# Opening a hand-synchronised section from ScalarE instead of SyncE in a batched matrix product

## The chip, the cores and the metric

The kernel runs on one NeuronCore of a Trainium2 chip. The metric is device time in microseconds (us) of one execution; for a series of runs the median is given. A profile of a single execution goes with it: its span runs from the first to the last instruction on the core.

## What is computed

Sixteen independent products of 512 x 512 matrices in float32, the first factor given transposed:

```
"a": np.random.randn(batch, k, m).astype(np.float32),     # batch = 16, k = m = n = 512
"b": np.random.randn(batch, k, n).astype(np.float32),
...
return np.matmul(a.transpose(0, 2, 1), b).astype(np.float32)
```

33.55 MB are read from HBM and 16.78 MB written.

## The kernel before

The batch is worked off in 8 pairs of 2 matrices. One pair of `a` (2 MB) or of `b` (2 MB) is one SBUF tile `x`; four such tiles (`NX = 4`) take turns. VectorE casts them to bfloat16 (`abf`, `bbf`, in two halves each), TensorE multiplies into four PSUM tiles (`ps`[...]), ScalarE copies PSUM to seven output tiles `o`, and these are stored to HBM. The first pair is treated specially: its first matrix alone is loaded in pieces of 256 KB and 768 KB per operand (lines 74 and 75), then the second in pieces of 1 MB (line 77), so that the first product can begin early. Its multiplications are those of line 135, all later ones those of line 155.

Nothing is left to the scheduler. All work of the five engines stands in one section, opened on line 72 by `tc.tile_critical`, in which every wait is written by hand on semaphores of the kernel's own (`s_x`, `s_cast`, `s_mm`, `s_ev`, `s_out` and so on). Within the section every engine runs its own list in order:

- SyncE issues all loads (lines 74 to 86) and the outputs of the first seven pairs (line 91), all on one DMA queue. The first eight loads wait for nothing; the later ones wait until VectorE is through with the tile (`s_in`). The outputs wait for the next to last load (`s_h`, line 88) and for ScalarE's `s_out` (line 90), so that stores come after the loads.
- VectorE: casts, lines 93 to 123.
- TensorE: two counted loops, lines 127 to 165.
- ScalarE: copies out of PSUM (lines 174 and 180) and a tiny write that raises `s_out` (line 185). The load of its function table, put in by the compiler, carries line 174 and is the first thing it does in the section.

The section itself has an opening and a closing. At the opening, one engine, the section's `sync_engine`, executes a NOP (line 72) that raises a semaphore, and every engine has a branch that waits for that semaphore before it enters. At the closing, the same engine raises another semaphore, each of the engines SyncE, ScalarE, VectorE and TensorE drains and reports, and the `sync_engine` collects the reports with semaphore waits and a last NOP, whose semaphore releases what comes after the section. No `sync_engine` is named on line 72, and the engine is SyncE then. Ahead of the opening lies a start barrier of all engines (line 207 in the profile); what follows the sections has line 218 (the end of the program's context).

After the section, a second one (line 188) with GpSimd as `sync_engine` waits for the outputs of the earlier pairs, and SyncE issues the output of the last pair (line 192). `tc.no_sync_barrier()` only keeps the order of the code; it makes no engine wait.

## Times and profile before

| quantity | before |
|---|---|
| median of 10 runs | 123.63 us (123.22 to 124.17) |
| the profiled execution | 123.62 us |
| its span | 121.9 us |
| mean granted TensorE clock | 0.854 |
| TensorE matmul busy | 62.2 us (51%) |
| VectorE busy | 38.0 us (31%) |
| ScalarE busy | 32.1 us (26%) |
| DMA, share of 16 engines | 97.6% |
| HBM traffic over the span | 413 GB/s |

How to read what is shown of the profile. Engines are PE (TensorE matmul), PEld (its weight load), DVE (VectorE), ACT (ScalarE), POOL (GpSimd), SP (SyncE); a "q" behind the name means the sequencer of that engine, which handles waits, branches, NOPs and the issue of DMAs, and isn't counted as busy. "L72" is line 72 of the kernel. The slices divide the span into 40 equal parts and give tenths of busy time. The chain that ended last goes back from the last instruction, each time to what released it. The timeline gives start and duration in us, and in brackets the idle time before and what ended it. In the views by stretches, the columns are named where they are shown.

### The profile page before, as it was taken

How to read it: one execution, taken by the hardware profiler on the slowest of the kernel's cores; microseconds unless marked ns; L12 is line 12 of the kernel's file. 1: busy time of each engine (PE TensorE's matmuls, PEld its weight loads, DVE VectorE, ACT ScalarE, POOL GpSimd, SP SyncE). 2: the span in 40 equal slices, each digit the busy share in tenths (PEclk: the TensorE clock that was granted, in tenths of full speed). 3: DMA queues.
4: the chain of work that ended last, by engine and by line, in shares of the span. 5: the costliest groups of instructions: out<-in, count | busy, mean ns of one | idle time of the engine just before them, and what ended most of it. 6: DMA issues, size and time to landing. Idle time of an engine off the chain costs nothing.

```text
span 121.9 us, 1209 instructions
## 1 busy us (share of the span) xinstructions
PE 62.2 (51%) x480; PEld 35.7 (29%) x480; DVE 38.0 (31%) x48; ACT 32.1 (26%) x41; POOL 0.2 (0%) x4
## 2 busy tenths in 40 slices
PE   0006928739969649979919928989900000000000
PEld 0002303326546334636606606646500000000000
DVE  0042070294494092474355437492000000000000
ACT  4000330510560830191570390191560000000000
POOL 0000000000000000000000000000000000000000
PEclk9999995999999995999999999999997555555555
DMA  3999999999999999999999999999999999999993
GB/s 95 365 425 428 468 430 430 430 430 430 430 430 430 430 430 430 430 430 436 430 430 430 436 430 401 422 430 428 428 428 430 430 428 428 428 428 430 430 428 161
DMA packets 5200, 50.33 MB, mean 413 GB/s; under 512 B 464, under 2 KB 464, under 8 KB 976
## 3 DMA queue, kind: packets, MB, share of 16 engines
q1 hardware_dynamic: 5200, 50.33, 97.6%
HBM read 33.55 MB, written 16.78 MB: 413 GB/s over the span
## 4 chain that ended last, share of the span: by engine, by line
DMA 51%; DVE 5%; PE 5%; ACT 3%; issue 2%; ACTq 0%; DVEq 0%
DMA x<-in_b_dram 36%; DMA x<-in_a_dram 9%; DMA out_dram<-o 6%; PE ps L135 5%; ACT o L180 3%; DVE bbf L117 2%; DVE abf L117 2%; DVE abf L98 1%; DVE done L123 0%; ACTq L72 0%; DVE bbf L98 0%; DVEq L116 0%
## 5 line engine op out<-in xcount | busy, mean ns | idle before, releaser
L155 PE MATMUL ps<-bbf,abf 64*128 64x512 bf16 x448 | 51.5, 386 | 12.9 <-PEq L150 12.9
L155 PEld LDWEIGHTS ps<-bbf,abf 64*128 64x128 bf16 x448 | 31.6, 112 | 32.8 <-issue 18.1
L180 ACT COPY o<-ps 128x1024 f32<-128x1024 f32 x28 | 26.3, 1027 | 38.9 <-PE ps L155 34.9
L117 DVE CAST abf<-x 128x2048 bf16<-128x2048 f32 x14 | 17.1, 1223 | 17.3 <-PE ps L155 11.9
L117 DVE CAST bbf<-x 128x2048 bf16<-128x2048 f32 x14 | 17.1, 1223 | 14.1 <-DMA x<-in_b_dram 14.1
L135 PE MATMUL ps<-bbf,abf 128*128 128x512 bf16 x32 | 10.7, 510 | 13.0 <-PEq L133 13.0
L135 PEld LDWEIGHTS ps<-bbf,abf 128*128 128x128 bf16 x32 | 4.1, 132 | 19.1 <-issue 18.0
L174 ACT COPY o<-ps 128x1024 f32<-128x1024 f32 x4 | 4.1, 1013 | 18.5 <-PE ps L135 18.5
L98 DVE CAST abf<-x 128x2048 bf16<-128x2048 f32 x2 | 2.5, 1226 | 12.0 <-PE ps L135 6.1
L98 DVE CAST bbf<-x 128x2048 bf16<-128x2048 f32 x2 | 2.4, 1224 | 1.6 <-DMA x<-in_b_dram 1.6
L185 ACT ACTIVATE done<-done 1x1 uint32<-1x1 uint32 x8 | 1.6, 197 | 0.0
L174 ACT ACT_TABLE_LOAD x1 | 1.3, 1283 | 0.9 <-SPq L72 0.9
L123 DVE MEMSET done<- 1x1 f32 x14 | 0.8, 59 | 0.0
L102 DVE MEMSET done<- 1x1 f32 x2 | 0.1, 59 | 0.0
L207 POOL MEMSET const-bfloat16-1.0<- 128x1 bf16 x1 | 0.1, 102 | 0.0
L207 POOL MEMSET const-uint8-127<- 128x1 uint8 x1 | 0.1, 102 | 0.0
L207 POOL MEMSET const-float32-1.0<- 128x1 f32 x1 | 0.1, 99 | 0.0
L207 POOL MEMSET const-float32-0.0<- 128x1 f32 x1 | 0.1, 98 | 0.2 <-issue 0.2
## 6 DMA issues: line engine op xcount, KB each, us to landing
out_dram<-o SPq DMA_DIRECT2D x8, 2048.0 KB, 21.8
x<-in_a_dram SPq DMA_DIRECT2D x7, 2048.0 KB, 12.1
x<-in_b_dram SPq DMA_DIRECT2D x6, 2048.0 KB, 15.9
x<-in_b_dram SPq DMA_DIRECT2D x3, 1024.0 KB, 13.5
x<-in_a_dram SPq DMA_DIRECT2D x1, 1024.0 KB, 8.4
x<-in_a_dram SPq DMA_DIRECT2D x1, 768.0 KB, 4.4
x<-in_b_dram SPq DMA_DIRECT2D x1, 768.0 KB, 6.4
x<-in_a_dram SPq DMA_DIRECT2D x1, 256.0 KB, 2.6
```

What stands on the lines that cost most here:

```text
L98: nc.vector.tensor_copy(out=bf_ts[0][:], in_=x_ts[j][:, u * RV:(u + 1) * RV, :]).then_inc(s_cast, 1)
L102: nc.vector.memset(dve_done[:, j:j + 1], 0.0).then_inc(s_in, 1)
L117: nc.vector.tensor_copy(out=(bbf_ts if n % 2 else abf_ts)[v][:], in_=x_ts[n % NX][:, v * RV:(v + 1) * RV, :],).then_inc(s_cast, 1)
L123: nc.vector.memset(dve_done[:, n:n + 1], 0.0).then_inc(s_in, 1)
L135: mm = nc.tensor.matmul(ps_ts[0][h][:, t % 2, :], a_m[:, r, t], bbf_ts[0][:, r, :], start=(r == 0), stop=(r == RV - 1),)
L155: mm = nc.tensor.matmul(ps_ts[g][h][:, t % 2, :], a_m[:, t], bbf_ts[v][rows, r, :], start=(v == 0 and r == 0), stop=(v == V - 1 and r == R ...
L174: nc.scalar.copy(out=o_ts[0][:, g, 2 * h:2 * h + 2, :], in_=ps_ts[0][h][:]).then_inc(s_ev[h], 1)
L180: ev = nc.scalar.copy(out=o_ts[i % NO][:, g, 2 * h:2 * h + 2, :], in_=ps_ts[g][h][:])
L185: nc.scalar.memzero(act_done[:, i:i + 1]).then_inc(s_out, 1)
L207: nc = _bacc.Bacc("TRN2", target_bir_lowering=False, num_devices=1)
```

## The change

One argument is added: the section's `sync_engine` is ScalarE (`EngineType.Activation`).

```diff
-    with tc.tile_critical(no_gpsimd_drain=True):
+    with tc.tile_critical(sync_engine=mybir.EngineType.Activation, no_gpsimd_drain=True):
         for j in range(2):
             nc.sync.dma_start(x_ts[j][:, 0:1, :], top_v[j]).then_inc(s_f[j], 16)
             nc.sync.dma_start(x_ts[j][:, 1:RV, :], low_v[j]).then_inc(s_f[j], 16)
```

## Prediction

> **What bounds the kernel now.** I read the granted clock and span first (one core, 121.9 us, clock 0.854), then the page's slices, then the chain that ended last, then the timeline of both ends of the span, and last the records of single instructions in the trace.

> The slices say that the DMA engines are the bound from about 2 us to 120 us.

> ```profile
> span 121.9 us, 1209 instructions
> ...
> PE 62.2 (51%) x480; PEld 35.7 (29%) x480; DVE 38.0 (31%) x48; ACT 32.1 (26%) x41; POOL 0.2 (0%) x4
> ...
> DMA  3999999999999999999999999999999999999993
> GB/s 95 365 425 428 468 430 430 430 430 430 430 430 430 430 430 430 430 430 436 430 430 430 436 430 401 422 430 428 428 428 430 430 428 428 428 428 430 430 428 161
> ...
> q1 hardware_dynamic: 5200, 50.33, 97.6%
> ```

> No compute engine is busy for more than half of the span, while the one DMA queue fills 97.6% of 16 engines. 50.33 MB at the steady 430 GB/s are 117.0 us of the 121.9. So the length is 117 us of transfer, plus what comes before the first packet, plus a slow ramp, plus the tail. Whatever moves the first packet moves everything behind it; whatever moves work that sits behind a full queue moves nothing.

> The first microseconds, from the timeline:

> ```profile
> 0.90 1.28 ACT L174 ACT_TABLE_LOAD   x1 [0.90 <-SPq L72]
> 0.94 0.39 SPq L74 DMA_DIRECT2D x<-in_a_dram  x1
> 1.39 0.42 SPq L75 DMA_DIRECT2D x<-in_a_dram  x1
> 1.86 0.42 SPq L74 DMA_DIRECT2D x<-in_b_dram  x1
> ```

> SyncE issues its first transfer at 0.94 us, and ScalarE was held until 0.90 by SyncE's line 72, the opening of the hand-made section. The two ends of the DMA stream, in stretches (columns: busy time of PE, PEld, DVE, ACT, POOL, then granted clock, DMA share, GB/s):

> ```profile
> 0.90:2.40 1.50, 0.00 (x0) 0.00 (x0) 0.00 (x0) 1.28 (x1) 0.00 (x0) 1.00 0.08 29
> 2.40:3.00 0.60, 0.00 (x0) 0.00 (x0) 0.00 (x0) 0.00 (x0) 0.00 (x0) 1.00 1.51 393
> 3.00:4.00 1.00, 0.00 (x0) 0.00 (x0) 0.00 (x0) 0.00 (x0) 0.00 (x0) 1.00 0.80 328
> 4.00:5.00 1.00, 0.00 (x0) 0.00 (x0) 0.00 (x0) 0.00 (x0) 0.00 (x0) 1.00 0.98 399
> 5.00:6.00 1.00, 0.00 (x0) 0.00 (x0) 0.14 (x1) 0.00 (x0) 0.00 (x0) 1.00 1.09 367
> 6.00:7.00 1.00, 0.00 (x0) 0.00 (x0) 1.00 (x1) 0.00 (x0) 0.00 (x0) 1.00 0.96 387
> 7.00:8.00 1.00, 0.00 (x0) 0.00 (x0) 0.08 (x1) 0.00 (x0) 0.00 (x0) 1.00 1.01 424
> ```

> Hardly a byte moves before about 2.2 us (first packet in the trace: 2.19), 1.25 us after the first issue. From there to 8 us the engines are never idle but below 430: 0.6 x 393 + 328 + 399 + 367 + 387 + 424 = 2,141 KB in 5.6 us, against 2,408 KB at 430, so 0.62 us is lost in the ramp.

> The close of the section, from the timeline of the end:

> ```profile
> 86.65 3.76 ACT o L180 x4
> 90.41 0.06 ACTq L72
> ...
> 90.60 3.64 SPq L192 DMA_DIRECT2D out_dram<-o  x1
> ```

> (the first two lines are the last of the chain). The last output is issued at 90.60 and lands, by the trace, 30.3 us later, at 120.93.

> [...]

> **The change part by part.** The records of the opening, in us from the span's start (not a view of the page, so given as I read them from the trace):

> ```
> 0.650 SP  semaphore wait (start barrier)    0.654 ACT the same
> 0.715 SP  NOP L72, 13 ns, raises the section's semaphore
> 0.751 ACT branch, waits for that semaphore
> 0.772 DVE branch, same    0.785 SP branch, same    0.812 PE branch, same
> 0.897 ACT table load      0.941 SP first DMA issue
> ```

> *Opening.* The change takes the NOP from SyncE and gives one to ScalarE; SyncE's branch then waits for ScalarE's semaphore. By SyncE's own spacing the NOP would fall on ScalarE 65 ns after its barrier wait: 0.654 + 0.065 = 0.719. SyncE's branch then comes when it hears of it. Three readings: as ScalarE heard SyncE (36 ns): 0.755; as GpSimd heard SyncE's NOP at the close (90.529 to 90.568, 39 ns): 0.758; as PE did (97 ns): 0.816. Against 0.785 that is -0.030, -0.027 or +0.031 us. SyncE can't come before 0.715, the place of its NOP, so the gain is at most 0.07 and, with the wait, 0.03. I take -0.03 us, because SyncE, like ScalarE and GpSimd, has short records (17 ns for a semaphore wait, PE 51). Bounds: -0.07 and +0.03. From branch to first issue (0.156 us) and from issue to issue (0.45 to 0.50 us) nothing changes, so all eight DMAs that follow (lines 74 to 83) move by the same amount, as does the first packet. This lies wholly on the path.

> *ScalarE's own part.* Its table load moves from 0.897 to about 0.95, by the extra NOP; it ends near 2.2, and the first copy (line 174) starts at 13.87, after 11.69 us of waiting for PE. Nothing, hidden by that wait; without the cover it would cost 0.05.

> *VectorE and PE.* Same instructions, released 4 ns later at 0.719. VectorE first works at 5.86, when data land; PE after that. Nothing.

> *Closing.* The gather of all engines moves too: ScalarE raises the closing semaphore, drains (1.089 us, started 89.415), then makes two semaphore waits and a NOP which now stand behind its own drain, where SyncE made its two waits beside it (89.587 and 89.646, NOP at 90.529). Two waits at some 0.06 us each and a hop to SyncE with its branch (0.04 to 0.15) put the issue of line 192 at about 90.8 to 90.9 in place of 90.60. Queued behind it on SyncE is only the final wait; GpSimd's line 188 also starts later by it, and then waits until 116.1 anyway. Its cover: six output transfers of 2 MB were still landing when line 192 was issued (outputs at about 91.5, 96.4, 101.3, 106.2, 111.1, 116.0), so 25 us of transfer stand ahead of it. Nothing, as long as the delay is below some 20 us; without cover it would cost 0.2 to 0.3.

> *Tail.* After the last landing (120.93) SyncE's last waits and the end barrier take 0.94 us, with the same kinds of waits; zero, bounds -0.07 and +0.07 (one wait more or less at the end).

> *Sum.* -0.03 us, with bounds -0.14 and +0.10. The profiled execution took 123.62 us, 121.87 of it span and 1.75 around it, which the change doesn't touch: 123.62 - 0.03 = 123.59. That execution is the median of the runs shown (123.63) to 0.01, so the forecast is 123.59. Differences under 0.2% (0.25 us) are about what a measurement of this kernel can tell from no change; the runs shown spread over 0.95 us, and a median of ten such can be off by 0.1 to 0.2.

> **The rivals.**
> *No effect:* SyncE hears of ScalarE as late as of itself, or as PE does: 123.62 to 123.65. For it: SyncE's branch came only 70 ns after its own NOP, and a hop has a price. Against: two hops of 36 and 39 ns.
> *The ramp falls out better:* another first moment gives another interleaving of the small first transfers (2 and 6 KB rows), and half of the 0.62 us is regained: 123.59 - 0.31 = 123.28. For it: the ramp is uneven (328, 399, 367 GB/s). Against: the order and spacing of the issues stay, and 30 ns is little beside 450.
> *Slower, ScalarE opens late:* ScalarE's lateness was covered by 11.69 us before; now each of its delays ahead of the NOP goes straight to the first DMA. It costs a measurable 0.25 us from the point where its NOP starts later than 0.719 + 0.03 + 0.25 = 1.00 us; if the table load (1.283 us) ran ahead of the NOP, SyncE's branch would come at 0.719 + 1.283 + 0.036 = 2.04, 1.25 later: 124.87. Against: in the changed program's order the NOP stands ahead of the table load, and ScalarE passed the start barrier 4 ns after SyncE. For: one execution is shown, and whether ScalarE is always so prompt isn't.

> **How the numbers follow.** Forecast 0.66, no effect 0.12, ramp better 0.14, ScalarE late 0.08. The forecast and "no effect" (0.78) are within 0.2%, but a draw of medians may carry about 0.06 of it past the bound downwards and 0.07 upwards. So faster 0.14 + 0.06 = 0.20; same 0.65; slower 0.08 + 0.07 = 0.15. The range 123.25 to 123.90 covers forecast, no effect and the better ramp with the spread of the medians; it leaves out the late ScalarE and some of the draws, less than 0.2.

> **What would show it.** In the changed profile: a NOP of line 72 on ScalarE's queue at about 0.72, none on SyncE; SyncE's branch near 0.755 and first issue near 0.91 (right), at 0.94 or later (no effect), beyond 1.2 (ScalarE late); the issues still 0.45 to 0.50 us apart; the stretch 2.4 to 8 us still near 2.14 MB, not 2.3; line 192 issued near 90.8 and still landing about 0.94 us before the span's end. The prediction is wrong if the span changes by more than 0.25 us with the first issue at 0.91.

## The result and the profile after

The changed kernel is slower, by about a third of a per cent.

| quantity | before | changed |
|---|---|---|
| median | 123.56 us (51 runs) | 123.87 us (14 runs) |
| ratio, with 95% interval | | 1.0033 [1.0018, 1.0047] |
| profiled execution | 123.62 us | 123.73 us |
| its span | 121.87 us | 121.64 us |
| the rest of its time, outside the span | 1.75 us | 2.09 us |

The last two lines hold the result: the profiled span became *shorter*, and the execution longer. What grew lies outside the part that the profile shows. The lines of the page of the changed kernel that answer to those shown of before:

```profile
span 121.6 us, 1210 instructions
...
PE 62.2 (51%) x480; PEld 35.0 (29%) x480; DVE 38.0 (31%) x48; ACT 32.1 (26%) x41; POOL 0.2 (0%) x4
...
DMA  3999999999999999999999999999999999999994
GB/s 75 403 422 426 458 431 431 431 431 436 431 431 431 431 431 431 431 431 431 431 431 431 431 431 399 431 428 428 428 426 428 431 426 426 431 426 420 428 428 189
...
q1 hardware_dynamic: 5200, 50.33, 97.9%
```

The DMA queue is as full as before (97.9% against 97.6%), at the same 430 GB/s or so. The opening, from the timeline of the changed kernel:

```profile
0.92 0.39 SPq L74 DMA_DIRECT2D x<-in_a_dram  x1
0.95 1.28 ACT L174 ACT_TABLE_LOAD   x1 [0.95 <-ACTq L72]
1.36 0.42 SPq L75 DMA_DIRECT2D x<-in_a_dram  x1
1.84 0.42 SPq L74 DMA_DIRECT2D x<-in_b_dram  x1
```

SyncE's first issue is at 0.92 (before: 0.94), and ScalarE now waits for its own line 72. What line 72 issues, by engine (columns: count, shortest, median and longest time in ns, first and last start in us), before:

```profile
L72 SPq EVENT_SEMAPHORE  x3: 17/17/28, 89.4 to 89.6; - x3
L72 SPq NOP  x2: 13/13/13, 0.7 to 90.5; - x2
```

and changed:

```profile
L72 ACTq EVENT_SEMAPHORE  x3: 17/17/38, 87.9 to 90.4; - x3
L72 ACTq NOP  x2: 14/14/14, 0.7 to 90.5; - x2
...
L72 ACTq DRAIN  x1: 2261/2261/2261, 88.0 to 88.0; - x1
L72 SPq DRAIN  x1: 123/123/123, 89.1 to 89.1; - x1
```

Both NOPs and the three semaphore instructions are ScalarE's now. With them, its compiled list has 59 instructions (waits, drains and branches counted) in place of 54; SyncE's has 47 in place of 51, since it also gets one wait more. So ScalarE's list grows by five and SyncE's shortens by four, where the section on the change named the two NOPs alone. (The profile records four of ScalarE's instructions fewer in each kernel, 50 and 55.) The end, from the timelines, before:

```profile
90.27 0.20 ACT L185 ACTIVATE done<-done 1x1 uint32<-1x1 uint32 x1
```

and changed:

```profile
90.06 0.20 ACT L185 ACTIVATE done<-done 1x1 uint32<-1x1 uint32 x1
90.54 3.44 SPq L192 DMA_DIRECT2D out_dram<-o  x1
```

Line 192 is issued 0.48 us after ScalarE's last write began; before, it was 0.33 us (90.27 to 90.60).

### The profile page after: what moved, and what is told of

Same layout as the page of the kernel before. It is cut to its first block, busy times and chain, and to the rows that moved or that the text cites. A ratio compares the mean times of both kernels' runs of the same rounds, so it can differ in the third digit from the quotient of the medians.

```text
span 121.6 us, 1210 instructions
## 1 busy us (share of the span) xinstructions
PE 62.2 (51%) x480; PEld 35.0 (29%) x480; DVE 38.0 (31%) x48; ACT 32.1 (26%) x41; POOL 0.2 (0%) x4
## 2 busy tenths in 40 slices
DMA packets 5200, 50.33 MB, mean 414 GB/s; under 512 B 464, under 2 KB 464, under 8 KB 976
## 3 DMA queue, kind: packets, MB, share of 16 engines
q1 hardware_dynamic: 5200, 50.33, 97.9%
## 4 chain that ended last, share of the span: by engine, by line
DMA 43%; DVE 7%; PE 3%; issue 3%; ACT 2%; ACTq 1%
DMA x<-in_b_dram 37%; DMA out_dram<-o 6%; DVE abf L117 4%; PE ps L135 3%; DVE bbf L117 3%; ACT o L180 2%; ACTq L72 1%; DVE done L123 0%; ACT done L185 0%
## 5 line engine op out<-in xcount | busy, mean ns | idle before, releaser
L155 PE MATMUL ps<-bbf,abf 64*128 64x512 bf16 x448 | 53.0, 394 | 12.9 <-PEq L150 12.9
L180 ACT COPY o<-ps 128x1024 f32<-128x1024 f32 x28 | 26.3, 1027 | 40.4 <-PE ps L155 36.4
L135 PE MATMUL ps<-bbf,abf 128*128 128x512 bf16 x32 | 9.2, 453 | 12.7 <-PEq L133 12.7
L174 ACT COPY o<-ps 128x1024 f32<-128x1024 f32 x4 | 4.1, 1015 | 16.7 <-PE ps L135 16.7
```

Source lines behind the costliest of these rows:

```text
L135: mm = nc.tensor.matmul(ps_ts[0][h][:, t % 2, :], a_m[:, r, t], bbf_ts[0][:, r, :], start=(r == 0), stop=(r == RV - 1),)
L155: mm = nc.tensor.matmul(ps_ts[g][h][:, t % 2, :], a_m[:, t], bbf_ts[v][rows, r, :], start=(v == 0 and r == 0), stop=(v == V - 1 and r == R ...
L174: nc.scalar.copy(out=o_ts[0][:, g, 2 * h:2 * h + 2, :], in_=ps_ts[0][h][:]).then_inc(s_ev[h], 1)
L180: ev = nc.scalar.copy(out=o_ts[i % NO][:, g, 2 * h:2 * h + 2, :], in_=ps_ts[g][h][:])
```

## The experiments

In all of them two parts of the time are kept apart: the span, and the run's time less its span, here called *outside*. The first varies from run to run by some tenths of a microsecond; the second is steady to 0.08 us, so that even one execution tells 1.75 from 2.10. Even these 0.08 us are mostly rounding, since the span of a run is on record to 0.1 us. For the profiled executions the exact span is kept, and outside is then 1.748 and 1.746 us for the kernel before and 2.088 and 2.087 us for the changed one. Theory A is that the loss lies outside, B that the DMA stream was drawn out (a ramp that fell out worse, where a rival of the prediction had it better), C that it was chance.

**The two kernels again, on one chip.** No edit.

> The kernel before, unchanged, as a control. It shows the spans of many executions of it, where so far only one was shown (span 121.9 us, 1.75 us of the 123.62 outside it). Theory A, that the change lengthened what lies outside the span: the median is 123.55 within 0.1, the part outside the span is 1.75 within 0.05 in every execution, and the spans are about 121.8. Theory B, that the DMA stream came out longer: the part outside varies between 1.7 and 2.1 here too, and the spans are shorter than the 121.8 of the changed kernel, near 121.4.

> The changed kernel, unchanged, beside the control on the same chip. Theory A: about 0.33 us slower than the control, all of it outside the span (2.07 against 1.75), spans the same to 0.05 us. Theory B: slower by as much in the span. Theory C, that the slower median was chance or another chip: within 0.1 us of the control.

Measured: before 123.39 us, ratio 0.9990 [0.9974, 1.0005]; changed 123.74 us, ratio 1.0024 [1.0006, 1.0041]; 0.35 us lie between the two. The control came out 0.16 us lower than expected, because its spans were shorter (121.73 us on average). Over the executions of this study, outside and the span are:

| | executions | outside: mean (range) | span: mean, standard error |
|---|---|---|---|
| before | 153 | 1.75 (1.67 to 1.82) | 121.83 +- 0.02 |
| changed | 30 | 2.10 (2.04 to 2.16) | 121.81 +- 0.06 |

The ranges of outside don't touch; the spans can't be told apart. A holds, B and C fall: the change costs 0.35 us, and all of it that can be measured lies outside the span. The first issue of the changed kernel is at 0.918 and 0.920 us in its two profiles.

**Another engine opens and closes.** In the one, VectorE; in the other, GpSimd.

```diff
-    with tc.tile_critical(sync_engine=mybir.EngineType.Activation, no_gpsimd_drain=True):
+    with tc.tile_critical(sync_engine=mybir.EngineType.DVE, no_gpsimd_drain=True):      # open_dve
+    with tc.tile_critical(sync_engine=mybir.EngineType.Pool, no_gpsimd_drain=True):     # open_pool
```

> VectorE instead of ScalarE opens and closes the section; SyncE has no NOP of its own ahead of its first DMA here either. If it is SyncE's shorter list that lengthens the part outside the span (theory A, SyncE's side), this kernel is 0.3 us slower than before as well, at about 123.9. If it is ScalarE's longer list (theory A, ScalarE's side), it is at 123.55. Theory B gives about 123.9, since SyncE's first issue comes earlier as in the changed kernel.

> GpSimd opens and closes the section. Theory A, SyncE's side: about 123.9, with 2.07 us outside the span. Theory A, ScalarE's side: about 123.55. Theory B: about 123.9, if SyncE's first issue is near 0.92 us in the profile.

Measured: VectorE 123.75 us, ratio 1.0015 [0.9994, 1.0037], outside 1.78; GpSimd 123.45 us, 0.9989 [0.9973, 1.0005], outside 1.76. Both have SyncE's short list of 47 instructions and ScalarE's old one of 54, and neither has the loss outside. So it isn't SyncE's shorter list. Nor is it the length of all lists together: those of ScalarE, SyncE and VectorE add up to 175 instructions in the changed kernel (59, 47, 69) and to 175 with VectorE as opener (54, 47, 74). ScalarE's side is left. GpSimd as opener gives the earliest first issue of all, from its timeline:

```profile
0.88 0.39 SPq L74 DMA_DIRECT2D x<-in_a_dram  x1
0.89 1.28 ACT L174 ACT_TABLE_LOAD   x1 [0.89 <-PEq L207]
```

0.06 us earlier than before; the median is lower by 0.10 us than its comparison, which the interval doesn't tell from nothing. (With VectorE as opener the median lay between the two that had been expected, because the spans were longer, 122.04 +- 0.08 us. Its first issue came at 0.96; the rest of that stays open.)

**ScalarE's length, without its role.** SyncE opens and closes as before; idle increments of a spare semaphore are put behind ScalarE's last write. As a counterpart (`after_less`), ScalarE opens and closes, but has less to do: `NO` is 7, so its work on the last pair is left out, and the output of that pair is not computed.

```diff
+    s_more = tc.alloc_semaphore("s_more")
...
             nc.scalar.memzero(act_done[:, i:i + 1]).then_inc(s_out, 1)
+        for _ in range(5):                      # or 1, 3, 7, 10, 14, 20
+            nc.scalar.sem_inc(s_more, 1)
```

```diff
-        for i in range(pairs):                  # after_less
+        for i in range(NO):
```

> The kernel before, SyncE as opener, with one idle semaphore increment (a spare semaphore) at the end of ScalarE's list, so 55 instructions on ScalarE instead of 54 (the changed kernel has 59). Looked at: the run's time less its span, 1.75 us before (1.68 to 1.82) and 2.10 changed (2.04 to 2.16). If each further instruction of ScalarE costs alike, 1.82; if a length is passed, 1.75 or 2.10; if it is ScalarE's role as opener and closer, 1.75.

> The same with three idle increments, 57 instructions on ScalarE. Each instruction alike: 1.96 us outside the span. A length passed: 1.75 or 2.10. ScalarE's role: 1.75.

> The same with five idle increments, 59 instructions on ScalarE, as many as in the changed kernel, but SyncE opens and closes. If ScalarE's length is the cause, in whatever form: 2.10 us outside the span. If ScalarE's role as opener and closer is: 1.75.

> The changed kernel, ScalarE as opener and closer, without ScalarE's work on the last pair (four copies, one write, one wait), so 53 instructions on ScalarE; the last pair's product is left out, and its place in the output gets an older one. If ScalarE's length is the cause: 1.75 us outside the span. If its role is: 2.10. The span is not looked at.

Measured outside: 1.77 with 55 instructions, 1.79 with 57, 2.11 with 59, and 1.77 for ScalarE as opener with 53. ScalarE's role is out as the cause, and the length of its list is in. It doesn't cost so much for each instruction: 0.04 us from 54 to 57, then 0.32 more at 59. The kernel with five increments, timed:

> The kernel before with five idle increments on ScalarE, timed. If ScalarE's length is the whole cause of the change's loss: slower than before by 0.35 us (ratio 1.003), with 2.10 us outside the span and a span within 0.1 us of before. If length is but a part: between 1.000 and 1.002.

Measured: 123.99 us, ratio 1.0030 [1.0016, 1.0044], outside 2.12 (22 executions), span 121.83 as before. Five idle instructions, with SyncE as opener, make the whole loss of the change. Its timeline shows that nothing else of the change is in it:

```profile
0.90 1.28 ACT L175 ACT_TABLE_LOAD   x1 [0.90 <-SPq L73]
0.94 0.39 SPq L75 DMA_DIRECT2D x<-in_a_dram  x1
```

(lines are one further down here): first issue at 0.94, ScalarE held by SyncE. In this execution TensorE let ScalarE begin its last pair 1.1 us later than in the profile of before (87.78 against 86.65), and the last output was issued at 91.72 us in place of 90.60, and the span (121.8 us) isn't longer for it: the cover that the prediction named held for 1.1 us.

**The changed kernel, shortened.** VectorE makes two of the last pair's copies, and the write that nobody waits for goes.

```diff
+        nc.vector.wait_ge(s_o0, 16)
+        for g in range(G):
+            nc.vector.wait_ge(s_mm, G * H * (pairs - 1) + g + 1)
+            nc.vector.tensor_copy(out=o_ts[(pairs - 1) % NO][:, g, 0:2, :], in_=ps_ts[g][0][:])
...
-            for h in range(H if i else 0):
+            for h in range(1 if i == pairs - 1 else 0, H if i else 0):
...
-            nc.scalar.memzero(act_done[:, i:i + 1]).then_inc(s_out, 1)
+            if i < pairs - 1:
+                nc.scalar.memzero(act_done[:, i:i + 1]).then_inc(s_out, 1)
```

> The changed kernel, ScalarE as opener and closer, with ScalarE's list cut to 56 instructions without leaving work out: VectorE, idle by then, makes two of the last pair's copies, and the last write of line 185, for which nothing waits, is dropped. If ScalarE's length alone is what made the change slow: 1.75 to 1.79 us outside the span, first issue still at 0.92, median 123.52, that is, the kernel before less 0.02 to 0.03 and not to be told from it. If the change costs by something else as well: 123.8 or more.

> The changed kernel without the last write of line 185, 58 instructions on ScalarE, between the 57 that had 1.79 us outside the span and the 59 that had 2.11. A sharp step gives one of these two values and so places it; a gradual rise gives about 1.95.

`after_58` has the last part of this edit alone. Measured: with 56 instructions 123.64 us, ratio 1.0010 [0.9988, 1.0032], outside 1.78; with 58 outside 1.90. The shortened kernel lost the 0.32 us outside; its median is 0.1 above the expected one, within the interval. 58 lies between the two values, in the one execution there is, so the rise doesn't look like one sharp step.

**Longer lists.** With SyncE as opener and 61, 64, 68 and 74 instructions on ScalarE, and the changed kernel with 61, 64 and 74 (2, 5 and 15 increments, put in as above).

> The kernel before with twenty idle increments on ScalarE, 74 instructions. If a length is passed once, after which it costs no more: 2.10 us outside the span. If from 58 on each instruction costs: above 2.3. [...] back to 1.75, perhaps with an instruction fetch inside the span in the DMA records.

> The kernel before with seven idle increments on ScalarE, 61 instructions. [...] 2.1 to 2.5 us outside the span. If the cost is confined to a few lengths about 59: 1.75.

> The same with ten idle increments, 64 instructions. A fetch still behind the span's end: 2.1 to 2.5 us outside it, or less where the fetch begins before the last barrier. A fetch inside the span, in its last microseconds or earlier: 1.75 to 1.8.

> The same with fourteen idle increments, 68 instructions. Fetch inside the span and 1.75 to 1.8 us outside, if the rule of 74 holds here; with a fetch behind the end, as at 59, 2.1 or more.

> The changed kernel with fifteen idle increments more on ScalarE, 74 instructions, the length at which the kernel before had its fetch of instructions inside the span. If the loss is the place of that fetch: 1.78 us outside the span, median 123.5 to 123.6, so that a longer list cures what a longer list had caused, and a fetch of 8192 bytes inside the span. If length as such or ScalarE's role adds to the loss: 2.1 or more, 123.9.

> The changed kernel with two idle increments more on ScalarE, 61 instructions. If the exact length of ScalarE's list decides, whoever opens the section: as the one look at 61 with SyncE as opener, 1.80 us outside the span, median about 123.55, not to be told from before. If that look was an accident and the loss spans the lengths from 59 to 64: 2.10, 123.9.

> The changed kernel with five idle increments more on ScalarE, 64 instructions. If the exact length decides: as the one look at 64 with SyncE as opener, 2.05 us outside the span, median 123.85, and a late fetch of instructions some 1.7 us behind the end. If that look was an accident: 1.80, 123.55.

All lengths together, outside in us (where there is one execution, from its exact span):

| instructions on ScalarE | SyncE opens | ScalarE opens |
|---|---|---|
| 53 | | 1.77 (one) |
| 54 | 1.75 (153) | |
| 55, 56, 57 | 1.77 (one), -, 1.79 (one) | -, 1.78 (14), - |
| 58 | | 1.90 (one) |
| 59 | 2.12 (22) | 2.10 (30) |
| 61 | 1.80 (one) | 1.75 (22) |
| 64 | 2.06 (one) | 1.96 (16; 1.81 to 2.12) |
| 68 | 1.80 (one) | |
| 74 | 1.78 (one) | 1.77 (14) |

The two columns agree row by row, to 0.05 us and, at 64, to within the spread: the number of ScalarE's instructions decides, and who opens the section doesn't. But it isn't a threshold, as the lengths up to 59 suggested: two more instructions than the changed kernel has (61) cost nothing. The changed kernel at 61 took 123.39 us, ratio 0.9988 [0.9973, 1.0004]; at 74, 123.55 us, 1.0007 [0.9989, 1.0026]; at 64, 123.84 us, 1.0017 [1.0003, 1.0031]. From the timeline at 61, which keeps the change's opening:

```profile
0.92 0.39 SPq L75 DMA_DIRECT2D x<-in_a_dram  x1
0.95 1.28 ACT L175 ACT_TABLE_LOAD   x1 [0.95 <-ACTq L73]
```

So the change's early first issue is there, two idle instructions are added, and the loss is gone.

**What I could see of why.** The DMA records hold some of the kind `instruction`, which I read as fetches of instructions. Those after the first microsecond have 8192 bytes each; by their start against the span's end:

```
before, changed, and 53 to 61         one, 0.63 to 0.91 us behind the end
64                                    two, 0.66 and 1.72 behind (SyncE opens), 0.93 and 1.71 (ScalarE)
68                                    two, 0.47 and 0.67 behind
74                                    one inside, at 95.2 (SyncE) and 96.0 (ScalarE), and one behind
VectorE's list 74 or 72 (else 69)     one inside, at 89.9 or 93.0, none behind
```

(74 on VectorE is the kernel that VectorE opens, 72 the shortened one, with 56 on ScalarE. The numbers 53 to 74 above them are ScalarE's.) With 64 and more on ScalarE there is a second fetch, and with 72 or 74 on VectorE the first lies inside the span. So when these fetches come depends on the lists' lengths, and at 64 the late fetch goes with a longer outside (2.06 and 1.96 us). But at 59, where the loss is largest (2.12 and 2.10 us), no second fetch is recorded, and at 61 neither; at 68, where the expectation had a fetch inside the span or else a loss, there are two behind it, and nothing is lost (1.80 us).

The traces also hold updates of semaphores behind the span's end, down to 1.9 us behind it. Before and changed, these come at the same moments to 0.015 us, the last one 1.872 and 1.873 us behind the end, so the 0.34 us is not in these steps; the last round of updates ahead of the span, which begins 0.370 and 0.371 us before it, doesn't hold it either. At 64 one block of updates (semaphores 54 to 104) begins late, at 1.245 us behind the end in both kernels in place of 0.79. A fetch has landed shortly before, at 1.21 and 1.24 us, but the last update of all comes at 1.92, where it is 1.89 and 1.92 at 61 without a loss. The traces don't show where the measured time begins and ends. That the loss is a fetch, and that it lies behind the kernel's end, was my guess; no run here shows either.

## Why the prediction was wrong

**The opening was right, and nearly in its size.** Predicted: NOP on ScalarE at 0.719, SyncE's branch at about 0.755, first issue near 0.91, table load at about 0.95. Measured: 0.723, 0.762, 0.918, 0.953. The term was -0.023 us in place of -0.03. The spans, 121.81 +- 0.06 against 121.83 +- 0.02, agree with it and can't show it.

**Closing: hidden, as predicted.** Line 192 came 0.15 us later after ScalarE's last write, in place of 0.2 to 0.3; that it was issued at 90.54 and not at 90.8 is because that write itself began 0.21 us earlier in this execution. In the kernel with five idle increments its issue was 1.1 us later altogether. Neither delay shows in the span.

**Tail: right within the span.** From the last landing (120.70) to the span's end it is 0.94 us, as before.

**The step that failed** is in the sum: "121.87 of it span and 1.75 around it, which the change doesn't touch". The change did touch it: 2.10. I had counted each instruction of the edit by what it does while it runs, and asked what hides it: the opening NOP as 0.05 us behind a wait of 11.69 us, the closing as 0.2 to 0.3 us behind the output transfers. ScalarE's list got five instructions longer by them, and its length was not a quantity of the sum at all. The time around the span thus stood in the sum with a change of nothing, without a reason; five idle instructions alone make it 2.12 us. By what step the length does this stays open. The bound for the unknown, -0.14 to +0.10, was drawn around the steps in the span only, with the tail's +-0.07; a term of +0.35 was outside it. The signs of being wrong, too, were all sought inside the span. That the measured 123.87 us lies in the range of 123.25 to 123.90 is luck: the range was made for the spread of medians and a better ramp, and nothing in it stood for this loss.

**The rivals.** *ScalarE opens late* had the right sign for a wrong reason: ScalarE's NOP came at 0.723. *The better ramp* seemed to come true in the first profile. In the stretch from 2.4 to 8 us (columns as in the prediction, the last is GB/s), before and changed:

```profile
2.40:8.00 5.60, 0.00 (x0) 0.00 (x0) 1.23 (x1) 0.00 (x0) 0.00 (x0) 1.00 1.03 382
```

```profile
2.40:8.00 5.60, 0.00 (x0) 0.00 (x0) 1.23 (x1) 0.00 (x0) 0.00 (x0) 1.00 1.01 401
```

The difference is worth 0.25 us at 430 GB/s (19 x 5.6 = 106 KB), which is about the 0.23 us by which this span was shorter. But the profile of before was the odd one: its first packet came at 2.19 us, the changed kernel's at 1.95. In the second pair of profiles the first packets came at 1.97 (before) and 1.93 (changed), and the same stretch moved 396 and 389 GB/s, the other way round. By their first packets (1.93, 1.95, 1.97 and 2.19 us) the four profiles moved 389, 401, 396 and 382 GB/s, so the rival's step from the first moment to the ramp isn't shown. The 30 spans show no gain either. *No effect* was wrong for the opening and right for the span, as far as the spans can tell.

## What to carry to other kernels

Compare the time and the span of the same execution before explaining a small difference: if the difference between them moved, as here from 1.75 to 2.10 us with the span at 121.8 in both, the waits and chains within the span don't hold the cause. Here five instructions more on ScalarE (59 for 54) cost 0.35 us outside the profiled span, and seven more (61) at most 0.05, by the exact length of its list. So where an edit adds a few instructions to one engine, try it with a few idle instructions more on that engine, and with another engine in the role, before judging the idea. A first issue that comes 0.02 us earlier, ahead of a stream that is full for 117 us, shows in the profiles and can't be measured in the total here, where the runs of one kernel spread over 1 us and more.

## What the runs showed of the hardware that I hadn't expected

- The time outside the span depends on the number of instructions on ScalarE and not evenly: 1.75 us at 54, 2.10 at 59, 1.75 at 61, 1.96 at 64, 1.77 at 74.
- It is very steady for one program, 1.67 to 1.82 us in 153 executions with the rounding of the spans in it, while the span of the same program varies by 1 us and more; the exception is 64, with 1.81 to 2.12.
- From the start of the opener's NOP to the start of SyncE's branch that waits for it, it took 39 ns from ScalarE (0.723 to 0.762) and 40 ns from GpSimd (0.686 to 0.726); SyncE's own NOP had held its branch for 70 ns.
- With 64 instructions on ScalarE, a block of semaphore updates behind the span's end begins 0.46 us later than before, at 1.245 us behind the end, whoever opens the section.
